# Mixer A's projections by 512 columns, indexer queries for 384 tokens, and the norm's squares shared with GpSimd

## The chip, the cores and the metric

The kernel runs on one core of a Trainium2 chip. What counts is the device time of one execution in microseconds (us). Three runs of the kernel before gave 1569.32, 1564.32 and 1567.81 us; the median is 1567.81 us. The core has five engines, each with its own queue of instructions: PE (TensorE: matmuls, and the transposes that are written as matmuls), DVE (VectorE), ACT (ScalarE), POOL (GpSimd) and SP (SyncE, which issues transfers here). PE's weight loads are shown apart from its matmuls, as PEld.

## The reference

Two layers of a transformer trunk on 512 tokens of width 1024, in fp32. Cut to what the change touches:

```
for l in range(2):
    h = rms_norm(x, norm_mix[l])                       # the "mixing norm"
    z = h @ w_in[l]
    qa, ka, va, qi, ki, wi, cq, ckv, kr, ga, gb = split_cols(z)
    # mixer A: 8 heads of 64; q and k are normed per head
    # indexer: I[t,s] = sum_h w[t,h] * relu(qi[t,h] . ki[s]); the best 128 keys of each query are kept
    y_a = sparse_indexed_attention(rms_norm(qa), rms_norm(ka), va, qi, ki, wi, rel_bias, topk=128)
    y_b = latent_attention(...)                        # mixer B: low-rank q and kv, 8 heads
    x = x + (sigmoid(ga) * (y_a @ w_proj_a) + sigmoid(gb) * (y_b @ w_proj_b)) @ w_out
    h = rms_norm(x, norm_ffn[l])
    x = x + (silu(gate) * val of causal_dwconv(h @ w_up)) @ w_down
```

A query of the first 128 tokens can see at most 128 keys, as many as are kept, so for these tokens the choice of the best keys leaves nothing out.

## The kernel before, in words

Each fp32 product is computed as three matmuls: both operands are split into a rounded high part and a low part (the rest), and the products high by high, low by high and high by low are summed in a PSUM bank. The activations' parts are called `hxh` and `hxl` (L295 on ACT, L296 on DVE).

**Weights** come as tiles of 128 rows and up to 1152 columns, in the order of one long list (`plan`). A tile passes through four steps: a transfer into `wr` (three buffers, issued by SP), the high part `wh` by a copy on ACT (L168), and the low part `wl`, either by a subtraction on DVE (L177) or, for the names in the set `DL`, by a negated copy on ACT (L193) and an accumulating transfer that POOL issues (L194). `wh` and `wl` have four buffers each. `get` hands out a tile's parts; `ahead`, called at the end of each tile's matmuls, starts the next tiles. The tiles `dn` of the down projection go through three more sums on POOL and DVE (L203 to L205), because the down projection is done with seven products of half the size instead of eight.

**A layer** is laid out around attention. The start of a layer is `lat`: the indexer queries in four tiles `qi` of 128 columns (two heads each), the first two of them interleaved by k while the norm's operands still arrive (L316 to L318), the next two through `dense` (L512), then `kiw` (the indexer's keys and head weights), `ckv` and `cq`. The evacuation of a `qi` tile (`stack`) is two copies on ACT (L301, L302) and two subtractions on DVE (L305, L306), and these free the PSUM bank. The mixing norm's sum of squares is made beside that: ACT squares the eight tiles of x (L446), DVE adds the squares up one after the other (L450), and four tiny matmuls on ones (L456) sum over the partitions; DVE's L461 goes on from there.

Then attention runs, first the indexer's scores and the choice of keys together with mixer B, then mixer A. Between its small steps PE gets *filler*: dense projections from a generator (`mix_dense`), handed out a few matmuls at a time at a rate set in the code; `later(n, f)` puts f off by n such steps. The filler's order is the order of the weight list: `gb`, `kv`, `uq`, then mixer A's projections `qa`, `ka`, `va` of heads 0 to 3 (`a0`), some `ga`, the same for heads 4 to 7 (`a1`), then `pb`, more `ga`, `pa`. `rows` computes a projection by token: the activations of 128 tokens are the stationary operand, and 256 columns of weights are streamed (L535). A weight tile holds four k slices of 256 columns; two PSUM banks take two token blocks each. There are 3 names x 2 groups x 96 = 576 such matmuls in a layer.

After mixer A come the output projection, the second norm, and the feed-forward in two halves: `uv` and `ug` (up projection, with the convolution), then `dn`. A group `mp` of down products ends with the residual sums: ACT's L1385, DVE's L1386 to L1392 write x. In layer 0 the next layer's first operands `hxh` wait for the last of them. A scheduler reorders the instructions of each engine from the traced program; the PSUM banks are D (2), L (3), T (2) and Y (1).

Of the kernel before, what the change touches and what calls it, by code (L numbers as in the profile page):

```python
# [10 lines left out]
F32 = mybir.dt.float32  # L11
# [8 lines left out]
D = 1024  # L20
# [8 lines left out]
TOPK = 128  # L29
IDX_SCALE = (8 ** -0.5) * (64 ** -0.5)  # L30
# [68 lines left out]
def dense_plan():  # L99
# [28 lines left out]
class Weights:  # L128


    def __init__(self, nc, wd, pool, slot, later):
# [8 lines left out]
        self.at = 2  # L140
# [13 lines left out]
    def split(self, i, lag=0):  # L154
        if i >= len(self.seq) or i in self.parts:
            return
# [12 lines left out]
        if name in DL:  # L169
            self.low_by_dma(t[:, :n], o[:, :n])  # L170
            return
# [42 lines left out]
    def ahead(self):  # L214

        for j in range(1, WB[1]):
            self.split(self.at + j, 2)
        for j in range(WB[1], WB[1] + WB[0] - 1):
            self.load(self.at + j)
        if PRE and self.at + WB[1] < len(self.seq) and self.seq[self.at + WB[1]][0] == "dn":  # L220
            self.sums(self.at + WB[1], self.raw[self.at + WB[1]])
# [3 lines left out]
def trunk(ctx: ExitStack, tc: tile.TileContext, xT, wd, vecs, rel, rot_n, onehot, outT):  # L225
# [72 lines left out]
    def stack(p, name):  # L298

        e, o = slot(name + "e", F32R), slot(name + "o", F32R)  # L300
        A.copy(e[0:64], p[0:64])  # L301
        A.copy(o[64:128], p[64:128])  # L302

        def low():
            V.tensor_tensor(out=e[64:128], in0=p[0:64], in1=e[0:64].bitcast(F32), op=OP.subtract)  # L305
            V.tensor_tensor(out=o[0:64], in0=p[64:128], in1=o[64:128].bitcast(F32), op=OP.subtract)  # L306
# [13 lines left out]
    def rsqrt(a, shape, quick=False):  # L320

        y, t = small("y", shape), small("t", shape)
# [88 lines left out]
    def late_consts():  # L411
# [7 lines left out]
        for n, w in ((0, 512), (1, 128)):  # L419
# [5 lines left out]
        nc.scalar.dma_start(bass.AP(tensor=dst.tensor, offset=dst.offset, ap=[[5120, 128], [640, 8], [1, 640]]),  # L425
                            bass.AP(tensor=src.tensor, offset=src.offset, ap=[[0, 128], [640, 8], [1, 640]]))
# [7 lines left out]
    class Norm:  # L434
        def __init__(self, gain):
            self.gain = gain
# [64 lines left out]
    def dense(kt, parts, xh, xl, evac, c0=0, last=True, tag="D"):  # L501
# [7 lines left out]
        for n, (w, x) in enumerate(seq):  # L509
            if n and n % 3 == 0:  # L510
                yield
            mm(p, lhsT=w, rhs=x, start=n == 0, stop=n == len(seq) - 1, skip_group_check=True)  # L512
# [5 lines left out]
    def rows(name, grp, nrm, evac):  # L518
# [1007 lines left out]
```

## Time and profile before

| | us |
|---|---|
| median of three runs | 1567.81 (1564.32 to 1569.32) |
| the profiled execution | 1562.11 |
| its span | 1560.4 |
| PE busy | 1542.9 (99%) |
| DVE busy | 1116.3 (72%) |
| ACT busy | 950.4 (61%) |
| POOL busy | 414.5 (27%) |

The profile is of one execution, whose time lies 1.7 us above its span. Busy shares are averages over a program in stages, so a table by stretches of the span says more than the whole. Matmuls overlap in PE's pipeline: the duration of a row is not what it costs. What a row of matmuls costs is the distance from one start to the next, called the cadence below. A note in brackets behind a row says how long the engine stood idle ahead of it and what it had waited for. The granted clock of TensorE is 1.00 in every stretch.

### The profile page before, as it was taken

Reading aid. Unit: us, or ns where it says so; the run is one execution under the profiler, and the core shown is the slowest. Engines: PE = TensorE matmul, PEld = TensorE weight load, DVE = VectorE, ACT = ScalarE, POOL = GpSimd, SP = SyncE. Lnnn points to the kernel's source line nnn. Section 1 sums busy time; section 2 is a strip of 40 time slices with the busy share of each in tenths; the row PEclk is TensorE's granted clock in tenths of the full one; section 3 lists DMA queues with packets and bytes.
Section 4 is the critical chain, followed back from the end, with each engine's and each line's share of the span. In section 5 each row is a group of like instructions: output and inputs, shape, how many; then the busy total and the mean of one; then the engine's idle time right before and its main releaser. Section 6 shows DMA issues by size and latency. Waiting matters only on the chain.

```text
span 1560.4 us, 23953 instructions
## 1 busy us (share of the span) xinstructions
PE 1542.9 (99%) x8662; PEld 1338.8 (86%) x8662; DVE 1116.3 (72%) x2271; ACT 950.4 (61%) x1551; POOL 414.5 (27%) x602
## 2 busy tenths in 40 slices
PE   9999999999999999999999999999999999999998
PEld 6888999888888898889978879998888888988898
DVE  7799988666476682548778999886574757735576
ACT  6757677773577545664457666687635764356642
POOL 1234003300011231217802430124000113412276
PEclk9999999999999999999999999999999999999999
DMA  7573134743578439983444732247435783499833
GB/s 238 150 183 96 55 95 100 184 126 118 128 187 190 109 106 212 215 190 88 142 149 110 171 97 62 84 123 174 145 98 140 185 190 94 114 209 209 198 101 102
DMA packets 72263, 221.11 MB, mean 142 GB/s; under 512 B 8448, under 2 KB 8744, under 8 KB 72016
## 3 DMA queue, kind: packets, MB, share of 16 engines
q1 hardware_dynamic: 53248, 149.41, 30.9%
q0 software_dynamic: 18432, 67.38, 23.3%
q10 hardware_dynamic: 464, 2.79, 0.6%
q8 instruction: 68, 1.11, 0.3%
q14 instruction: 51, 0.42, 0.1%
HBM read 143.77 MB, written 6.84 MB: 97 GB/s over the span
## 4 chain that ended last, share of the span: by engine, by line
PE 69%; DVE 10%; POOL 4%; DMA 4%; ACT 3%; issue 2%; POOLq 0%; DVEq 0%; ACTq 0%; SPq 0%
PE D L512 37%; PE T L512 14%; PE D L535 6%; DMA wr<-in_wd_dram 2%; PE Y L1033 2%; POOL wr L205 2%; PE T L1026 2%; DVE wl L188 2%; DMA wl<-wr 1%; PE L L1373 1%; POOL wr L204 1%; PE L L313 1%; POOL wr L203 1%; PE L L312 1%; ACT wh L183 1%
## 5 line engine op out<-in xcount | busy, mean ns | idle before, releaser
L168 ACT CAST wh<-wr 128x1024 fp32r<-128x1024 f32 x202 | 211.9, 1051 | 177.7 <-PE D L512 67.1
L194 POOL DMA_DIRECT2D wl<-wr x128 | 110.8, 873 | 646.4 <-ACT wl L193 596.3
L512 PE MATMUL D<-hxh,wh 128*128 128x512 f32 x464 | 185.2, 399 | 0.4 <-DVE qio L306 0.4
L512 PE MATMUL D<-hxl,wh 128*128 128x512 f32 x464 | 183.5, 396 | 0.0
L183 ACT CAST wh<-wr 128x896 fp32r<-128x896 f32 x88 | 82.8, 942 | 127.4 <-POOL wr L205 99.5
L193 ACT ACTIVATE wl<-wr 128x1024 fp32r<-128x1024 f32 (+1 forms) x128 | 135.7, 1060 | 26.6 <-PE D L512 19.6
L205 POOL TENSOR_TENSOR wr<-wr 128x256 f32<-128x256 f32 x88 | 108.1, 1228 | 92.1 <-DVE wr L204 76.6
L188 DVE TENSOR_TENSOR wl<-wr,wh 128x896 fp32r<-128x896 f32 x88 | 102.0, 1160 | 40.4 <-ACT wh L183 36.0
L1068 POOL TENSOR_TENSOR P<-M,sel 128x128 f32<-128x128 f32 (+1 forms) x64 | 54.4, 903 | 274.4 <-DMA M<-skewd 229.7
L512 PE MATMUL D<-hxh,wl 128*128 128x512 f32 x464 | 126.1, 397 | 0.0
L535 PE MATMUL D<-wh,hxh 128*128 128x256 f32 x384 | 114.0, 298 | 0.0
L535 PE MATMUL D<-wl,hxh 128*128 128x256 f32 x384 | 108.9, 284 | 0.0
L535 PE MATMUL D<-wh,hxl 128*128 128x256 f32 x384 | 108.4, 283 | 0.0
L512 PEld LDWEIGHTS D<-hxh,wh 128*128 128x128 f32 x464 | 87.5, 189 | 15.7 <-issue 0.8
L177 DVE TENSOR_TENSOR wl<-wr,wh 128x1024 fp32r<-128x1024 f32 x74 | 92.0, 1246 | 11.5 <-ACT wh L168 9.2
L512 PEld LDWEIGHTS D<-hxl,wh 128*128 128x128 f32 x464 | 87.4, 188 | 14.4
L512 PE MATMUL D<-hrl,wh 128*128 128x512 f32 x256 | 99.6, 389 | 0.0
L512 PE MATMUL D<-hrh,wh 128*128 128x512 f32 x256 | 99.6, 389 | 0.0
L512 PE MATMUL T<-hrh,wh 128*128 128x512 f32 x256 | 99.6, 389 | 0.0
L512 PE MATMUL T<-hrl,wh 128*128 128x512 f32 x256 | 99.6, 389 | 0.0
L512 PEld LDWEIGHTS D<-hxh,wl 128*128 128x128 f32 x464 | 84.4, 188 | 15.4 <-issue 0.2
L293 DVE TENSOR_TENSOR ptl<-T,pth 128x512 fp32r<-128x512 f32 (+3 forms) x128 | 60.9, 484 | 21.8 <-ACT pth L292 20.7
(395 smaller groups left out, 4516.5 us busy)
## 6 DMA issues: line engine op xcount, KB each, us to landing
wr<-in_wd_dram SPq DMA_DIRECT2D x198, 512.0 KB, 4.1
wl<-wr POOLq DMA_DIRECT2D x124, 512.0 KB, 5.6
wr<-in_wd_dram SPq DMA_DIRECT2D x88, 256.0 KB, 2.7
x<-in_xT_dram SPq DMA_DIRECT2D x16, 256.0 KB, 4.2
M<-skewd SPq DMA_DIRECT2D x16, 256.0 KB, 4.0
skewd<-biasd ACTq DMA_DIRECT2D x1, 2560.0 KB, 13.6
wr<-in_wd_dram SPq DMA_DIRECT2D x4, 576.0 KB, 3.9
wl<-wr POOLq DMA_DIRECT2D x4, 576.0 KB, 6.1
```

The lines of the kernel that those rows point to most:

```text
L168: self.nc.scalar.copy(h[:, :n], t[:, :n])
L177: eng.tensor_tensor(out=o[:, c], in0=t[:, c], in1=h[:, c].bitcast(F32), op=OP.subtract)
L183: self.nc.scalar.copy(h[:, :896], t[:, 128:1024])
L188: self.later(lag, lambda: self.nc.vector.tensor_tensor(out=o[:, :896], in0=t[:, 128:1024], in1=h[:, :896].bitcast(F32), op=OP.subtract))
L193: self.nc.scalar.activation(o, t, AF.Copy, scale=-1.0)
L194: self.nc.gpsimd.dma_start(o.bitcast(F32), t, accum_op=OP.add)
L205: g(2)(out=b[:, 6:8], in0=b[:, 0:3:2], in1=b[:, 3:6:2], op=OP.add)
L293: later(lag, lambda: V.tensor_tensor(out=o, in0=src, in1=h.bitcast(F32), op=OP.subtract))
L512: mm(p, lhsT=w, rhs=x, start=n == 0, stop=n == len(seq) - 1, skip_group_check=True)
L535: mm(pp[b][:, t, :], lhsT=x, rhs=w, start=n == 0 and half == 0 and t == 0, stop=n == 11 and half == 1, skip_group_check=True)
L1026: nc.tensor.transpose(p[:, (i - j) * 128:(i - j + 1) * 128], P[:, P0[i] + j * 128:P0[i] + (j + 1) * 128], ident)
L1068: G.tensor_tensor(out=P[:, P0[i]:P0[i] + w], in0=M[:, 512 - w:512], in1=sel[:, SEL0[i]:SEL0[i] + w], op=OP.add)
```

## The change

1. `rows` streams 512 columns. The weights are packed anew: `qk` holds q and k of four heads (2 x 256 columns), four tiles of two k slices; `va` holds v of all heads and is made once. All four tiles of a projection are fetched ahead of its first matmul, a PSUM bank takes one token block, and the tiles are given back during the last of the four token blocks. A layer has 3 x 96 = 288 such matmuls. `a0` is now `qk` and `va`, `a1` is `qk` alone.
2. The indexer queries are made for tokens 128 to 511: 384 columns a matmul (192 matmuls over both layers), and `stack` copies 384 columns.
3. The mixing norm's squares 5 to 7 are added to square 4 on POOL, which also adds the two sums; DVE keeps the adds of squares 1 to 3.
4. The transfer of the bias table `skewd` (2560 KB, issued by ACT) is put off by 36 steps.
5. The first two tiles behind a run of `dn` tiles (`uv` and `ug` with index 10, in each layer) get their low part from DVE.
6. `held`: at the last two pairs of tiles of the group mp = 3, in layer 0, the next tiles' work is written behind the residual sums instead of ahead of them.
7. The per-head norm of mixer A's q and k is one chain of [128, 4, 8] per group of heads instead of two of [128, 16] (q, k).

```diff
-    for g in range(2):
-        p += [(n, 2 * g + half, 1024) for n in ("qa", "ka", "va") for half in range(2)]
-        if g == 0:
-            p += [("ga", m, 1024) for m in range(GA_0)]
+    p += [("qk", i, 1024) for i in range(4)] + [("va", i, 1024) for i in range(4)]
+    p += [("ga", m, 1024) for m in range(GA_0)]
+    p += [("qk", 4 + i, 1024) for i in range(4)]
...
-        if name in DL:
+        if name in DL and not any(self.seq[j][0] == "dn" for j in (i - 1, i - 2)):
...
-    def rows(name, grp, nrm, evac):
-        pp = [bank("D").rearrange("p (t c) -> p t c", t=2) for _ in range(2)]
-        for half in range(2):
-            h, o = W.get(name, 2 * grp + half)
-            for b in range(2):
-                for t in range(2):
...
+    def rows(name, i0, nrm, evac):
+        parts = [W.get(name, i0 + i) for i in range(4)]
+        for t in range(4):
+            p = bank("D")
+            ts = slice(t * 128, (t + 1) * 128)
+            for i, (h, o) in enumerate(parts):
+                c = lambda k: slice(k * 512, (k + 1) * 512)
+                xs = [(nrm.h[2 * i + k][:, ts], nrm.o[2 * i + k][:, ts]) for k in range(2)]
+                seq = [(x, h[:, c(k)]) for k in range(2) for x in xs[k]] + [(xs[k][0], o[:, c(k)]) for k in range(2)]
+                for n, (x, w) in enumerate(seq):
+                    if n == 3:
+                        yield
+                    mm(p, lhsT=x, rhs=w, start=i == 0 and n == 0, stop=i == 3 and n == 5, skip_group_check=True)
+                if t == 3:
                     W.ahead()
...
-                mm3(p, h, o, nrm.h[k], nrm.o[k], k == 0, k == KD - 1)
+                mm3(p[:, T_IDX:], h, o, nrm.h[k][:, T_IDX:], nrm.o[k][:, T_IDX:], k == 0, k == KD - 1)
...
-                later(lag, lambda: V.tensor_tensor(out=self.acc, in0=self.acc, in1=q, op=OP.add))
+                def add():
+                    if k < 4 or not self.two:
+                        V.tensor_tensor(out=self.acc, in0=self.acc, in1=q, op=OP.add)
+                    else:
+                        G.tensor_tensor(out=self.acc2, in0=self.acc2, in1=q, op=OP.add)
+                    if k == KD - 1 and self.two:
+                        G.tensor_tensor(out=self.acc, in0=self.acc, in1=self.acc2, op=OP.add)
+                later(lag, add)
...
-                W.ahead()
+                held = last and mp == 3 and l < DEPTH - 1 and kp in pairs[-2:]
+                if held:
+                    W.split(W.at + 1, 2)
+                else:
+                    W.ahead()
...
+            if held:
+                W.ahead(2)
```

What the scheduler makes of it, at three places. The first is PE's queue at the norm's sum in layer 0, first before, then after. `D_402` (after: `D_401`) is the bank of `kiw`, `D_334` that of the fourth `qi` tile, `relb` is the operand of the bias table, and the matmuls on `ones` are the norm's sum.

```order
L512 MATMUL D_334<-hxh_175,wl_198 128x512
L421 MATMUL T_362<-oh_356,relb 8x512
L421 MATMUL T_366<-oh_357,relb 8x128
L512 MATMUL D_334<-hxh_179,wl_198 128x512
...
L512 MATMUL D_402<-hxh_143,wh_308 128x512
...
L512 MATMUL D_402<-hxl_160,wh_308 128x512
L456 MATMUL T_410<-ones,sq_228 128x1 x4
```

```order
L528 MATMUL D_333<-hxh_187,wl_198 128x384
L528 MATMUL D_401<-hxh_143,wh_307 128x512
...
L528 MATMUL D_401<-hxh_171,wh_307 128x512
L427 MATMUL T_362<-oh_356,relb 8x512
L427 MATMUL T_366<-oh_357,relb 8x128
L528 MATMUL D_401<-hxl_172,wh_307 128x512
L528 MATMUL D_401<-hxh_175,wh_307 128x512
L528 MATMUL D_401<-hxl_176,wh_307 128x512
L472 MATMUL T_409<-ones,sq_228 128x1 x4
```

The bias table's matmuls moved from the tail of the last `qi` tile into `kiw`, and the norm's sum comes after ten matmuls of `kiw` instead of six. It now waits for POOL, whose queue after the change has these rows at that place (`sq_228` is the sum, `sq_290` the second sum).

```order
L463 TENSOR_TENSOR sq_290<-sq_290,sq_298 128x512
L463 TENSOR_TENSOR sq_290<-sq_290,sq_328 128x512
L463 TENSOR_TENSOR sq_290<-sq_290,sq_343 128x512
L465 TENSOR_TENSOR sq_228<-sq_228,sq_290 128x512
L597 TENSOR_TENSOR w_81_502<-wn_500,r_82_503 128x32
```

On DVE's queue in layer 0 four of the seven adds are gone, and the low part of a third weight tile now stands ahead of the subtractions that free the second-last `qi` bank, where before it stood behind them.

The second place is ACT's queue at the boundary from layer 0 to layer 1, first before, then after. `t_8294` (after: `t_7963`) is the first of the last residual sums, `hxh` are the next layer's operands; the numbers of the names grow in the order in which the code asks for buffers.

```order
L168 CAST wh_8196<-wr_8138 128x1024
L168 CAST wh_8224<-wr_8170 128x1024
L168 CAST wh_8262<-wr_8199 128x1024
L168 CAST wh_8289<-wr_8227 128x1024
L1385 COPY t_8294<-D_8108 128x256
L295 ACTIVATE hxh_8304<-x_4394,vec 128x512
```

```order
L168 CAST wh_7876<-wr_7818 128x1024
L168 CAST wh_7904<-wr_7850 128x1024
L168 CAST wh_7981<-wr_7879 128x1024
L168 CAST wh_7984<-wr_7907 128x1024
L1394 COPY t_7963<-D_7788 128x256
L297 ACTIVATE hxh_7973<-x_4076,vec 128x512
```

The names show that the two last casts are now asked for behind the residual sum (7981 and 7984 against 7963), but they stand where they stood. The same holds on DVE for their low parts, and on SP for the transfers. The transfer of the bias table has moved by one row of ACT's queue: it stood one row ahead of a weight cast and now stands one row behind it.

The third place is ACT's queue behind the first half's `dn` tiles in layer 0, first before, then after. `wr_6332` and `wr_6376` (after: `wr_6023`, `wr_6058`) are the `uv` and `ug` tiles with index 10.

```order
L183 CAST wh_6373<-wr_6301 128x896
L168 CAST wh_6400<-wr_6332 128x1024
L193 ACTIVATE wl_6401<-wr_6332 128x1024
L168 CAST wh_6428<-wr_6376 128x1024
L193 ACTIVATE wl_6429<-wr_6376 128x1024
L168 CAST wh_6456<-wr_6405 128x1024
L193 ACTIVATE wl_6457<-wr_6405 128x1024
```

```order
L184 CAST wh_6055<-wr_6021 128x896
L168 CAST wh_6082<-wr_6023 128x1024
L168 CAST wh_6109<-wr_6058 128x1024
L168 CAST wh_6136<-wr_6085 128x1024
L194 ACTIVATE wl_6137<-wr_6085 128x1024
```

Two negated copies are gone from ACT, and with them two accumulating transfers from POOL's queue; DVE has two subtractions more there.

Elsewhere on PE the filler moves with the shorter projections: in layer 0 mixer B's last scores end at row 991 of PE's queue instead of 1119, mixer A's first scores begin at row 1062 instead of 1166, and the eight score matmuls of mixer A's last head, which had filler between them, stand together at rows 1530 to 1537, with `pb` behind them.

## Rows read from the trace of the kernel before

**Rows 1.** The page's part 1: busy time, share of the span, instructions.

```profile
PE 1542.9 (99%) x8662; PEld 1338.8 (86%) x8662; DVE 1116.3 (72%) x2271; ACT 950.4 (61%) x1551; POOL 414.5 (27%) x602
```

**Rows 2.** Busy time by stretches of the span; last clock, DMA share, GB/s.

```profile
core 0: us, PE busy (x) PEld busy (x) DVE busy (x) ACT busy (x) POOL busy (x), PEclk, DMA share, GB/s
61.00:184.00 123.00, 121.76 (x674) 103.96 (x672) 120.69 (x350) 81.30 (x166) 34.70 (x85) 1.00 0.47 118
184.00:274.00 90.00, 89.21 (x705) 86.15 (x705) 75.80 (x187) 66.95 (x143) 17.20 (x19) 1.00 0.35 94
760.00:794.00 34.00, 30.24 (x196) 26.17 (x195) 25.89 (x33) 15.49 (x21) 15.29 (x17) 1.00 0.57 186
```

**Rows 3.** Two stretches, of line L535 (the projections by token) alone.

```profile
184.00:274.00 90.00, 68.94 (x480) 61.72 (x480) 1.00 0.35 94
960.00:1049.00 89.00, 68.96 (x480) 61.82 (x480) 1.00 0.34 91
```

**Rows 4.** Timeline of PE: start, duration; matmuls of 256, 512 and 384 columns.

```profile
232.08 0.28 PE L535 MATMUL D<-wh,hxl 128*128 128x256 f32 x1
...
233.04 0.28 PE L535 MATMUL D<-wh,hxh 128*128 128x256 f32 x1
...
335.20 0.39 PE L512 MATMUL D<-ybl,wh 128*128 128x512 f32 x1
...
336.11 0.39 PE L512 MATMUL D<-ybl,wh 128*128 128x512 f32 x1
...
107.73 0.33 PE L844 MATMUL L<-wl,cqh 128*128 128x384 f32 x1
...
108.59 0.33 PE L844 MATMUL L<-wh,cql 128*128 128x384 f32 x1
```

**Rows 5.** Timeline of PE at the start of layer 0.

```profile
11.61 0.50 PE L317 MATMUL L<-hxl,wh 128*128 128x512 f32 x1 [0.28 <-DVE hxl L296]
...
18.36 0.39 PE L512 MATMUL D<-hxh,wh 128*128 128x512 f32 x1
...
28.65 1.24 PE L421 MATMUL T<-oh,relb 32*8 32x512 f32 x4
...
30.62 0.39 PE L512 MATMUL D<-hxh,wh 128*128 128x512 f32 x1
...
31.99 0.95 PE L456 MATMUL T<-ones,sq 128*128 128x1 f32 x8
32.80 0.49 PE L512 MATMUL D<-hxh,wh 128*128 128x512 f32 x1
```

**Rows 6.** Timeline of DVE at the start of layer 0.

```profile
28.55 0.69 DVE L306 TENSOR_TENSOR qio<-D,qio 64x512 fp32r<-64x512 f32 x1
...
30.42 0.68 DVE L450 TENSOR_TENSOR sq<-sq,sq 128x512 f32<-128x512 f32 x1
```

**Rows 7.** Timeline of PE at the boundary of the layers.

```profile
791.81 0.50 PE L316 MATMUL L<-hxh,wh 128*128 128x512 f32 x1 [1.70 <-ACT hxh L295]
...
806.71 0.47 PE L512 MATMUL D<-hxh,wh 128*128 128x512 f32 x1 [0.40 <-DVE qio L306]
```

**Rows 8.** Timeline of ACT at the boundary of the layers.

```profile
791.03 1.33 ACT L295 ACTIVATE hxh<-x,vec 128x512 fp32r<-128x512 f32 x2 [4.54 <-DVE x L1389]
...
803.51 0.63 ACT L446 ACTIVATE sq<-x 128x512 f32<-128x512 f32 x1
```

**Rows 9.** Timeline of PE behind the `dn` tiles of both layers.

```profile
590.52 1.65 PE L512 MATMUL D<-hrh,wl 128*128 128x512 f32 x6 [0.80 <-DMA wl<-wr]
...
1366.46 1.88 PE L512 MATMUL D<-hrh,wl 128*128 128x512 f32 x7 [0.59 <-DMA wl<-wr]
```

**Rows 10.** Groups of instructions by line and shape: busy, mean ns, idle before.

```profile
L631 POOL TENSOR_TENSOR sqc<-sqc,sqc 128x512 f32<-128x512 f32 x2 | 3.0, 1476 | 0.0
...
L450 DVE TENSOR_TENSOR sq<-sq,sq 128x512 f32<-128x512 f32 x28 | 19.3, 688 | 0.7 <-ACT sq L446 0.2
```

**Rows 11.** The page's part 5, columns as in rows 10: a weight tile's two splits.

```profile
L168 ACT CAST wh<-wr 128x1024 fp32r<-128x1024 f32 x202 | 211.9, 1051 | 177.7 <-PE D L512 67.1
...
L177 DVE TENSOR_TENSOR wl<-wr,wh 128x1024 fp32r<-128x1024 f32 x74 | 92.0, 1246 | 11.5 <-ACT wh L168 9.2
```

**Rows 12.** The page's part 6, DMA issues: KB each, median us to landing.

```profile
wr<-in_wd_dram SPq DMA_DIRECT2D x198, 512.0 KB, 4.1
wl<-wr POOLq DMA_DIRECT2D x124, 512.0 KB, 5.6
```

More of the change, by code (lines that the diff above doesn't have):

```diff
@@ L212, in get, with ahead @@
         return self.parts.pop(i)
-    def ahead(self):
+    def ahead(self, n=1):
+        self.used += n
         for j in range(1, WB[1]):
-            self.split(self.at + j, 2)
+            self.split(self.used + j, 2)
         for j in range(WB[1], WB[1] + WB[0] - 1):
-            self.load(self.at + j)
-        if PRE and self.at + WB[1] < len(self.seq) and self.seq[self.at + WB[1]][0] == "dn":
-            self.sums(self.at + WB[1], self.raw[self.at + WB[1]])
+            self.load(self.used + j)
+        if PRE and self.used + WB[1] < len(self.seq) and self.seq[self.used + WB[1]][0] == "dn":
+            self.sums(self.used + WB[1], self.raw[self.used + WB[1]])
 @with_exitstack
@@ L320, in rsqrt @@
     def rsqrt(a, shape, quick=False):
-        y, t = small("y", shape), small("t", shape)
+        if int(np.prod(shape)) > 16:
+            y, t = (sb.tile([128] + shape, F32, name=nm("y"), tag="heads", bufs=4) for _ in range(2))
+        else:
+            y, t = small("y", shape), small("t", shape)
         V.tensor_scalar(y.bitcast(I32), a.bitcast(I32), -0.5, float(0x5F3759DF), op0=OP.mult, op1=OP.add)
@@ L434, in trunk, with __init__ @@
     class Norm:
-        def __init__(self, gain):
-            self.gain = gain
+        def __init__(self, gain, two=False):
+            self.gain, self.two = gain, two
             self.h, self.o = [None] * KD, [None] * KD
@@ L498, in spread, with dense @@
             A.copy(row, p)
-    def dense(kt, parts, xh, xl, evac, c0=0, last=True, tag="D"):
+    def dense(kt, parts, xh, xl, evac, c0=0, last=True, tag="D", t0=0):
         h, o = parts
@@ L706, in mix_dense, with heads, evac @@
         done.add("latent")
-        def heads(name, grp, gain):
-            ss = small("ss", [16])
+        def heads(grp, gain):
+            ss = sb.tile([128, 4, 8], F32, name=nm("ss"), tag="heads", bufs=4)
             nat = []
-            def evac(b, p):
-                p = p.rearrange("p t c -> p (t c)")
+            def evac(t, p):
                 r, q = slot("raw"), slot("sqa")
@@ L745, in turn @@
                 hd = 4 * grp + 2 * pr
-                if gain is None:
-                    st["qa"][hd:hd + 2] = stack(p, name)
+                if not keys:
+                    st["qa"][hd:hd + 2] = stack(p, "qa")
                     return
@@ L1375, in down @@
                         tick()
-                W.ahead()
+                held = last and mp == 3 and l < DEPTH - 1 and kp in pairs[-2:]
+                if held:
+                    W.split(W.at + 1, 2)
+                else:
+                    W.ahead()
                 tick()
```

109 lines of the change are left out of this document (50 added, 59 removed).

## The prediction

> **What bounds the kernel.** I read the page's part 1 first: PE is busy for 1542.9 us of the span [rows 1], so time can only come from three places: matmuls that cost less, the few stalls between them, or stretches in which PE only fills the time of another engine. Then the table by stretches tells these apart [rows 2]. In 184 to 274 us PE is busy for 89.21 of 90 us and DVE for 75.80: PE is the limit. In 61 to 184 us (choice of keys, mixer B) DVE is busy for 120.69 of 123 us: PE's filler is free cover there, and a matmul less saves nothing by itself. In 760 to 794 us (boundary of the layers) PE has 30.24 of 34 us; a chain of waits decides. Last came the timeline, for the distance between starts of matmuls [rows 4]: 256 columns 0.120 us ((233.04 - 232.08) / 8), 384 columns 0.172 us (0.86 / 5), 512 columns 0.2275 us (0.91 / 4). The cost per column falls only a little with more columns.
>
> **The projections by token.** They stream the same columns in half as many matmuls. Two of 256 cost 0.240 us, one of 512 costs 0.2275 us: 12.5 ns for each pair. The change counts where PE is the limit. The two such stretches hold 480 of a layer's 576 instructions each [rows 3]; the other 96 lie where DVE is the limit and give nothing. So 2 x 240 x 12.5 ns = 6.0 us is saved. If the 96 count too it is 7.2 us.
>
> A rule bears on this and would make the term smaller. The rows show 12.5 ns a pair [rows 4]. The Trainium skill (TensorE: Matmul & The Clock Gate, Back-to-back issue gap) puts the isolated distance of warm matmuls at columns / 2.4 plus 2.5 ns, by which 256 and 512 columns take 109.2 and 215.8 ns, and a pair saves 2.5 ns: an estimate by that page is 1.2 us instead of 6.0. The trace's distances lie above both figures, and the smaller form lies further above; I keep the rows.
>
> The new form asks for four tiles at once. Each tile takes ACT 1.05 us and DVE 1.25 us [rows 11]. The tiles are given back one by one in the last token block, 6 x 0.2275 = 1.4 us apart, so the splits of the next four can follow at that pace, and the first has 18 x 0.2275 = 4.1 us from its release to its use, against 2.3 us for the two splits. I cost this at nothing; the cover is the raw tile already landed, and what it costs without that is a rival below.
>
> The shorter filler shifts all that follows, as the order shows: mixer A's last head has no filler between its eight scores. PE would then wait for a bank to be freed now and then. The nearest row is a wait of 0.40 us for DVE to free a bank [rows 7]; two in a layer are 0.8 us. From 0 to 1.5 us a layer is possible; I add 1.5 us for both.
>
> **The indexer queries.** 96 matmuls a layer go from 512 to 384 columns, 55 ns each: 5.3 us a layer at most. At the start of layer 0 not all of it is worth something. PE waits for the operands' low parts until 11.61 us [rows 5]; of the first 48 matmuls some 28 stand behind that wait, and with the 48 of the next two tiles 76 x 55 ns = 4.2 us are saved by the time `kiw` begins. It would then begin at 30.62 - 4.2 = 26.4 us [rows 5], and 1.2 us earlier still since the bias table's matmuls (1.17 us) have moved into it. But it needs the bank that DVE's subtraction frees at 28.55 + 0.69 = 29.24 us [rows 6]. There DVE has three adds of 0.69 us less ahead and one split of 1.25 us more [rows 10, 11]: 28.4 us. From 28.4 us `kiw` takes 24 x 0.2275 = 5.5 us, the norm's sum 0.8 us and the bias table 1.2 us: it ends at 35.9 us. Before, it ended at 30.62 + 5.5 + 0.8 = 36.9 us. So layer 0 saves **1.0 us**; bounds are 0 and 4.2.
>
> At layer 1 the operands of the last two k slices come late: PE waits 1.70 us for `hxh` at 791.81 us [rows 7], and this operand ends a chain through ACT and DVE in which ACT idles 4.54 us for the last residual sum [rows 8]. All that PE saves ahead of it is waited away. Behind it stand 12 of the first 48 matmuls (0.7 us). Then `kiw` begins at 806.71 us, after a wait for DVE [rows 7], in whose queue three adds ahead go away: 2.1 us earlier. Together 2.7 us, less half of a possible wait of 0.8 us for the norm's sum (next paragraph): **2.3 us**, bounds 0.7 and 5.3.
>
> **The squares.** Eight of DVE's adds (0.69 us each) become eight of POOL's, for which 1.48 us is the nearest row [rows 10]. DVE's gain is in the bank's release above. The chain's end moves: after the last square, POOL needs up to two adds, 3.0 us. In layer 1 the last square ends at 803.51 + 0.63 = 804.1 us [rows 8], perhaps 0.9 us earlier now, so the sum is ready near 806.2 to 807.1 us, and the norm's sum, ten matmuls into `kiw`, comes at 804.4 + 2.3 = 806.7 us. In layer 0 it comes at 28.4 + 2.3 + 1.2 = 31.9 us; DVE's last add began at 30.42 us [rows 6], and POOL's ends near 31.4. Behind it on PE stands the rest of `kiw`. Hence the 0.4 us charged in layer 1. If POOL's adds take longer, PE waits by as much.
>
> On the chip's side: the Trainium skill (GPSIMD Engine Reference, Key points) says that GpSimd shares its interfaces to SBUF with VectorE and that instructions with two SBUF inputs contend; the adds have two each. No row here shows such an add beside DVE's splits, so that is left to a rival.
>
> **The tiles after `dn`.** PE waits for the accumulating transfer at 590.52 us (0.80 us) and at 1366.46 us (0.59 us) [rows 9]. The chain is ACT's copies and a transfer of 5.6 us [rows 12]; DVE's subtraction takes 1.25 us [rows 11]. I count the whole **1.4 us**; DVE's queue behind the residual sums could keep half.
>
> **The rest at nothing.** `held` changes no row of ACT's, DVE's or SP's order at the boundary, so the late operand there stays late. The bias table's transfer moves one row. The shorter norm per head saves DVE some short instructions where PE is the limit.
>
> **The sum.** -6.0 - 1.0 - 2.3 - 1.4 + 1.5 = -9.2 us. The profiled execution took 1562.1 us, 5.7 us under the median 1567.8 us of the runs shown. It becomes 1552.9 us; put against the median, **1558.6 us**.
>
> **The rivals.**
> - *Every matmul counts.* The filler in the stretches of DVE and the queries at both starts all shorten the way: 7.2 + 10.6 + 1.4 = 19.2 us, 1548.6 us. For it: PE is busy for 99%. Against it: three waits by name in rows 5 and 7.
> - *The starts take all of the queries' gain.* POOL's adds run 1 us longer each, as the norm's sum then waits, or the bank is freed no earlier: -6.0 - 1.4 + 1.5 = -5.9 us, 1561.9 us.
> - *Wider matmuls give nothing much.* The distance between starts would be set by columns alone, so that two of 256 cost nearly one of 512: PE's rows of 256 columns would shrink to their share whatever their number. The rows at 232 us speak against it, though they stand in a mixed stretch. With 1.2 us for the projections in place of 6.0 the sum is -4.4 us: 1563.4 us. This is the skill's rule above (TensorE: Matmul & The Clock Gate), as a mechanism.
> - *The moved work acts as written.* If the two casts did run behind the residual sums, PE's 1.70 us wait and the other stalls of a stretch with 30.24 of 34 us busy shrink [rows 2], by up to 4 us: 1555 us. The order speaks against it.
> - *Slower: four tiles at once starve PE.* Where a tile has not landed when its block begins, transfer (4.1 us [rows 12]) and splits (1.05 + 1.25 us) lie bare, 6.4 us. There are three blocks a layer, and the tiles behind them. To undo the sum and reach slower, six starts would have to lose (9.2 + 4.7) / 6 = 2.3 us each. At half of 6.4 us each the loss is 19.2 us: 1567.8 - 9.2 + 19.2 = 1577.8 us. For it: DVE is busy for 84% of that stretch (75.80 of 90, [rows 2]), so that its splits queue. Against it: the releases above, and transfers at a share of 0.35.
>
> **Chances and range.** A measurement tells about 0.3%, 4.7 us, from no change: 1563.1 to 1572.5 us. The forecast 0.52 (its own range 1554 to 1562), every matmul 0.10, moved work 0.05, the starts take all 0.15 (a fifth of it within 0.3%), wider matmuls little 0.08 (on the bound; within), starved PE 0.10 (0.03 within, 0.07 slower). Faster: 0.52 + 0.10 + 0.05 + 0.12 - 0.03 for the scatter of runs = 0.76; within 0.17; slower 0.07. The range leaves out most of the starved case and little else: 1548 to 1566 us.
>
> **What would show it.** The projections' starts 0.2275 us apart in a stretch shorter by 3 us a layer; `kiw` beginning near 28.4 us and 2 us earlier behind the boundary; no wait for `wl` behind the `dn` tiles; the wait for `hxh` at the boundary still there, and longer. The prediction is wrong if rows of `wh` or `wl` from ACT and DVE appear as PE's waits at the first matmul of a projection, if the norm's sum waits for POOL by over 2 us, or if the stretch of mixer A does not shorten though its matmuls do.

## The result and the profile after

Nine runs of the changed kernel had a median of 1577.11 us (1571.41 to 1581.13), nine of the kernel before 1567.81 us (1562.73 to 1571.94). The ratio is 1.0068, with a 95% interval of 1.0055 to 1.0081: 9.3 us slower by the medians, where 9.2 us faster was forecast. The profiled execution took 1575.77 us with a span of 1572.9 us, 12.5 us more than before. The two profiles are not alike in their luck: that of before (1562.11 us, its mean granted clock 1.000) is faster than each of the nine runs, that of after lies near the median. So the table below shows where time is lost, and overstates by some 3 us how much.

The page's part 1 after the change [rows 1]:

```profile
PE 1540.0 (98%) x8086; PEld 1310.1 (83%) x8086; DVE 1105.4 (70%) x2223; ACT 945.8 (60%) x1547; POOL 425.6 (27%) x606
```

PE has 576 instructions less and hardly less busy time. Part of its busy time ran at half the clock, and the rest of the loss is idle time. To find the places I took the same landmarks in both timelines: the first index score, the first projection of mixer A's output (the `ya` matmuls), the start of layer 1, and the same in layer 1.

| from, to | before, us | after, us | difference |
|---|---|---|---|
| 0, first index score | 45.56 | 49.57 | +4.0 |
| first index score, first `ya` (attention) | 313.86 | 319.72 | +5.9 |
| first `ya`, layer 1 (output, feed-forward) | 421.17 | 418.42 | -2.8 |
| layer 1, first index score | 39.79 | 38.97 | -0.8 |
| first index score, first `ya` | 314.80 | 321.72 | +6.9 |
| first `ya`, last matmul | 419.33 | 418.65 | -0.7 |

**The start of layer 0.** PE's timeline after the change (start, duration, in brackets the idle ahead) answers to [rows 5]:

```profile
28.42 0.47 PE L528 MATMUL D<-hxh,wh 128*128 128x512 f32 x1 [2.40 <-DVE qio L309]
...
29.20 0.39 PE L528 MATMUL D<-hxl,wh 128*128 128x512 f32 x1
29.42 0.58 PE L528 MATMUL D<-hxh,wh 128*128 128x512 f32 x1
29.80 0.63 PE L528 MATMUL D<-hxl,wh 128*128 128x512 f32 x1
...
30.79 2.30 PE L427 MATMUL T<-oh,relb 32*8 32x512 f32 x4
...
34.46 1.70 PE L472 MATMUL T<-ones,sq 128*128 128x1 f32 x8
...
37.02 0.63 PE L528 MATMUL D<-hxh,wh 128*128 128x512 f32 x1
37.45 0.63 PE L528 MATMUL D<-hxl,wh 128*128 128x512 f32 x1
...
41.03 0.39 PE L528 MATMUL D<-hxh,wh 128*128 128x512 f32 x1
```

`kiw` begins at 28.42 us, and waits 2.40 us for the bank, as worked out (28.4 us). But behind 29.8 us the starts of such matmuls lie 0.43 us apart (37.02 and 37.45 us) instead of 0.23. The table by stretches (PE, PEld, DVE, ACT and POOL busy, then granted clock, DMA share, GB/s) shows why:

```profile
15.00:25.00 10.00, 10.00 (x60) 10.00 (x59) 8.64 (x11) 9.13 (x16) 4.67 (x7) 1.00 0.51 163
25.00:29.00 4.00, 1.60 (x9) 1.22 (x9) 3.23 (x4) 2.74 (x5) 2.25 (x2) 1.00 0.74 217
29.00:31.00 2.00, 2.00 (x7) 1.05 (x6) 1.35 (x1) 0.32 (x1) 1.92 (x2) 0.62 0.86 330
31.00:39.00 8.00, 8.00 (x22) 5.39 (x21) 2.45 (x14) 1.71 (x5) 0.82 (x1) 0.50 0.24 75
39.00:41.00 2.00, 2.00 (x8) 1.58 (x8) 0.83 (x3) 1.01 (x1) 0.00 (x0) 0.82 0.60 164
41.00:46.00 5.00, 5.00 (x25) 4.14 (x24) 1.62 (x2) 1.57 (x3) 0.00 (x0) 1.00 1.03 283
```

Behind the idle the granted clock is 0.50, the lower of TensorE's two levels, for about ten us. In that stretch a busy share of 100% hides the loss: what a matmul costs is read from the starts and the clock.

**Attention.** PE has two waits of over 1 us in each layer here. The first is where the last projection `qk` begins, shown on DVE and then on PE:

```profile
237.50 1.23 DVE L178 TENSOR_TENSOR wl<-wr,wh 128x1024 fp32r<-128x1024 f32 x1 [0.76 <-ACT wh L168]
...
239.47 1.23 DVE L178 TENSOR_TENSOR wl<-wr,wh 128x1024 fp32r<-128x1024 f32 x1
...
241.21 1.22 DVE L178 TENSOR_TENSOR wl<-wr,wh 128x1024 fp32r<-128x1024 f32 x1
242.35 1.65 DVE L298 SCALAR_TENSOR_TENSOR va<-D,rstd,va 128x256 fp32r<-128x256 f32 x4
```

```profile
243.36 0.47 PE L547 MATMUL D<-wh,hxh 128*128 128x512 f32 x1 [1.27 <-DVE va L298]
```

DVE is given the low parts of the next four tiles in a burst, and three of them stand ahead of the subtractions that empty the two banks of `va`. The second wait is behind that projection, when the first `ga` tiles are wanted (in both kernels all of `ga` follows the last projection, and `pb` follows `ga`). First come POOL's accumulating transfer for the first `ga` tile with its time to landing and SP's next two issues, then ACT's queue, then PE's:

```profile
266.94 0.86 POOL L195 DMA_DIRECT2D wl<-wr  x1 [9.93 <-ACT pth L294]
```

```profile
wl<-wr POOLq DMA_DIRECT2D x1, 512.0 KB, 4.6
```

```profile
271.56 0.33 SPq L151 DMA_DIRECT2D wr<-in_wd_dram  x1
...
274.73 0.33 SPq L151 DMA_DIRECT2D wr<-in_wd_dram  x1
```

```profile
270.17 1.06 ACT L194 ACTIVATE wl<-wr 128x1024 fp32r<-128x1024 f32 x1
...
277.54 1.04 ACT L168 CAST wh<-wr 128x1024 fp32r<-128x1024 f32 x1 [4.35 <-DMA wr<-in_wd_dram]
278.49 1.05 ACT L194 ACTIVATE wl<-wr 128x1024 fp32r<-128x1024 f32 x1
279.45 0.60 ACT L352 ACTIVATE P<-P,mx 128x384 f32<-128x384 f32 x1
279.96 0.19 ACT L352 ACTIVATION_READ_ACCUMULATOR P<-P,mx 128x1 f32 x1
280.05 0.56 ACT L294 CAST pth<-T 128x512 fp32r<-128x512 f32 x1
```

```profile
280.66 0.50 PE L1038 MATMUL Y<-pth,va 128*128 128x512 f32 x1 [3.48 <-ACT pth L294]
...
282.29 0.63 PE L528 MATMUL D<-hxl,wh 128*128 128x512 f32 x1
```

ACT's cast of the fourth `ga` tile waits 4.35 us for its transfer, issued only at 271.56 us, when the accumulating transfer that read the first tile's raw buffer had landed (266.94 us and 4.6 us). Behind that cast in ACT's queue stand the negated copy of the same tile, an exponent of the softmax and the cast `pth` that PE needs. The list of waits names `pth`; the cause stands four rows higher. PE idles for 3.48 us, and from 281.9 to 285.1 us its starts too lie 0.43 us apart.

**The boundary** answers to [rows 7]:

```profile
799.23 0.62 PE L319 MATMUL L<-hxh,wh 128*128 128x384 f32 x2 [3.67 <-ACT hxh L297]
...
812.06 0.47 PE L528 MATMUL D<-hxh,wh 128*128 128x512 f32 x1 [2.06 <-ACT qio L305]
...
814.36 1.05 PE L472 MATMUL T<-ones,sq 128*128 128x1 f32 x8 [0.68 <-POOL sq L465]
```

The wait for `hxh` is 3.67 us instead of 1.70, and `kiw` waits for its bank here too. The clock stays at 1.00 behind both in this execution. That is the exception: in the profiles of e1 to e4, e6 to e9 and e11 below, PE waits 2.85 to 4.46 us here and the clock falls during or behind each of these waits. So it is in e1 (the row of the wait, and 798 to 802 us at 0.50):

```profile
796.79 0.69 PE L319 MATMUL L<-hxh,wh 128*128 128x384 f32 x1 [3.44 <-ACT hxh L297]
```

```profile
798.00:802.00 4.00, 4.00 (x14) 4.00 (x13) 2.05 (x4) 2.47 (x4) 0.00 (x0) 0.50 0.00 0
```

### The profile page after: what moved, and what is told of

Its sections match the earlier page's. It is cut to its first block, busy times and chain, and to the rows that moved or that the text cites. A ratio compares the mean times of both kernels' runs of the same rounds, so it can differ in the third digit from the quotient of the medians.

```text
span 1572.9 us, 22741 instructions
## 1 busy us (share of the span) xinstructions
PE 1540.0 (98%) x8086; PEld 1310.1 (83%) x8086; DVE 1105.4 (70%) x2223; ACT 945.8 (60%) x1547; POOL 425.6 (27%) x606
## 4 chain that ended last, share of the span: by engine, by line
PE 72%; DVE 7%; POOL 5%; issue 4%; DMA 3%; ACT 2%; SPq 0%; POOLq 0%; DVEq 0%; ACTq 0%
PE D L528 36%; PE T L528 15%; PE D L547 4%; PE L L1378 3%; PE Y L1038 2%; PE T L1378 2%; PE T L1031 2%; POOL wr L206 2%; DMA wr<-in_wd_dram 2%; PE D L1378 1%; PE L L528 1%; PE Y L1378 1%; POOL wr L205 1%; POOL wr L204 1%; DVE wl L178 1%
## 5 line engine op out<-in xcount | busy, mean ns | idle before, releaser
L195 POOL DMA_DIRECT2D wl<-wr x124 | 107.4, 866 | 691.9 <-ACT wl L194 608.4
L528 PE MATMUL D<-hxh,wh 128*128 128x512 f32 (+1 forms) x464 | 186.7, 402 | 4.5 <-DVE qio L309 2.4
L528 PE MATMUL D<-hxl,wh 128*128 128x512 f32 (+1 forms) x464 | 185.1, 399 | 0.0
L194 ACT ACTIVATE wl<-wr 128x1024 fp32r<-128x1024 f32 x124 | 131.7, 1062 | 34.2 <-PE D L528 20.1
L206 POOL TENSOR_TENSOR wr<-wr 128x256 f32<-128x256 f32 x88 | 114.5, 1302 | 90.5 <-DVE wr L205 83.0
L528 PE MATMUL D<-hxh,wl 128*128 128x512 f32 (+1 forms) x464 | 125.5, 395 | 0.0
L178 DVE TENSOR_TENSOR wl<-wr,wh 128x1024 fp32r<-128x1024 f32 x78 | 97.6, 1258 | 13.2 <-ACT wh L168 8.7
L547 PE MATMUL D<-wh,hxh 128*128 128x512 f32 x192 | 78.7, 410 | 2.5 <-DVE va L298 2.5
L1324 DVE SCALAR_TENSOR_TENSOR c<-T,vec,c 128x511 f32<-128x511 f32 x32 | 23.9, 748 | 80.2 <-ACT c L1321 80.2
L547 PE MATMUL D<-wh,hxl 128*128 128x512 f32 x192 | 77.9, 406 | 0.0
```

Source lines behind the costliest of these rows:

```text
L178: eng.tensor_tensor(out=o[:, c], in0=t[:, c], in1=h[:, c].bitcast(F32), op=OP.subtract)
L194: self.nc.scalar.activation(o, t, AF.Copy, scale=-1.0)
L195: self.nc.gpsimd.dma_start(o.bitcast(F32), t, accum_op=OP.add)
L206: g(2)(out=b[:, 6:8], in0=b[:, 0:3:2], in1=b[:, 3:6:2], op=OP.add)
L528: mm(p[:, t0:], lhsT=w, rhs=x[:, t0:], start=n == 0, stop=n == len(seq) - 1, skip_group_check=True)
L547: mm(p, lhsT=x, rhs=w, start=i == 0 and n == 0, stop=i == 3 and n == 5, skip_group_check=True)
```

## The experiments

Two causes are to be told apart from others: at the start, an idle that the shorter queries open, and a clock that falls behind it; in attention, the burst of weight tiles. Each experiment was timed in five rounds against the kernel before, whose own median was 1565.59 us beside e1 to e4, 1566.20 us beside e5 to e8 and 1567.04 us beside e9 to e12; so ratios are compared, not medians. The intervals of e1, e2, e5, e6, e8 and e11 overlap that of the changed kernel: what these show, they show by the waits, the landmarks and the clock of one profile each. In the table "score" is the time of layer 0's first index score in the profile (45.56 us before the change, 49.57 after), and "clock" that of the stretch from 31 to 39 us.

| run | median, us | ratio to before, 95% interval | score | clock |
|---|---|---|---|---|
| changed kernel | 1577.11 | 1.0068 (1.0055 to 1.0081) | 49.57 | 0.50 |
| e1 cover | 1574.30 | 1.0052 (1.0039 to 1.0066) | 45.46 | 1.00 |
| e2 `kiw` in bank Y | 1580.46 | 1.0090 (1.0074 to 1.0105) | 51.29 | 0.63 |
| e3 `ga` by DVE | 1568.06 | 1.0012 (0.9999 to 1.0026) | 49.67 | 0.50 |
| e4 old projections | 1563.05 | 0.9980 (0.9967 to 0.9993) | 45.42 | 1.00 |
| e5 queries of 512 | 1575.10 | 1.0054 (1.0036 to 1.0072) | 45.70 | 1.00 |
| e6 sum on PE | 1573.65 | 1.0043 (1.0026 to 1.0060) | 49.37 | 0.57 |
| e7 e4 and e6 | 1564.49 | 0.9989 (0.9975 to 1.0003) | 47.38 | 0.79 |
| e8 `uv` as before | 1576.62 | 1.0062 (1.0040 to 1.0085) | 50.50 | 0.50 |
| e9 e3 and e5 | 1565.33 | 0.9993 (0.9982 to 1.0004) | 46.10 | 1.00 |
| e10 e4 and e5 | 1560.61 | 0.9967 (0.9953 to 0.9980) | 45.65 | 1.00 |
| e11 squares on DVE | 1577.65 | 1.0068 (1.0053 to 1.0084) | 49.64 | 0.50 |
| e12 `uv` alone | 1562.26 | 0.9971 (0.9959 to 0.9983) | 46.26 | 1.00 |

**e1, cover.** Matmuls without use fill the idle ahead of `kiw`.

```diff
+        if l == 0:
+            pw = bank("Y")
+            for k in range(10):
+                mm(pw, lhsT=wi[1][:, k % 8 * 128:k % 8 * 128 + 128], rhs=nrm.h[k % 8], start=True, stop=True)
         yield from dense(KD, W.get("kiw", 0), nrm.h, nrm.o, lambda p: nrm.after(lambda: evac_kiw(p)))
```

> Ten more matmuls of 512 columns into an unused bank stand ahead of kiw in layer 0; their results are not used. They fill the 2.40 us in which PE waited for kiw's bank at 26.0 us; kiw can begin no earlier than before. Theory (the idle lowered the granted clock): the clock stays at full speed behind 28.4 us, the first index score comes near 45.5 us instead of 49.57 us, and the time falls by about 4 us against the changed kernel, to about 1573 us (ratio to the kernel before near 1.004). Rival (the clock fell for another reason, such as the transfers or the small bias-table matmuls): the first index score stays near 49.5 us and the time near 1577 us. Neither expects anything of mixer A.

PE's timeline in e1, and the stretch that was at 0.50:

```profile
25.01 2.47 PE L714 MATMUL Y<-hxh,wl 128*128 128x512 f32 x10
27.41 1.24 PE L427 MATMUL T<-oh,relb 32*8 32x512 f32 x4
28.58 0.50 PE L528 MATMUL D<-hxh,wh 128*128 128x512 f32 x1
```

```profile
31.00:39.00 8.00, 7.18 (x36) 6.11 (x37) 4.50 (x17) 1.82 (x3) 0.76 (x1) 1.00 0.88 281
```

`kiw` begins no earlier (28.58 us), the clock stays at 1.00, and the score comes 4.1 us earlier although more work was added. The ratio falls by 0.0016, or 2.5 us, which is not clear of the noise; the span of the profile is only 0.9 us shorter, since the clock falls at the boundary here (above). The bias table's matmuls also stand ahead of `kiw` here, which the edit did not aim at.

**e2, `kiw` in bank Y**, so that no wait for DVE is left.

```diff
-        yield from dense(KD, W.get("kiw", 0), nrm.h, nrm.o, lambda p: nrm.after(lambda: evac_kiw(p)))
+        yield from dense(KD, W.get("kiw", 0), nrm.h, nrm.o, lambda p: nrm.after(lambda: evac_kiw(p)), tag="Y")
```

> The changed kernel with kiw's sum in the bank tagged Y instead of D, in both layers, so that kiw needs no bank freed by DVE. Theory (the bank's release is what PE waits for, and the clock falls behind that idle): kiw begins at 26.1 us instead of 28.4 us, the clock stays at full speed, the first index score comes near 42.5 us instead of 49.57 us; at layer 1 the 2.06 us wait at 812.06 us is gone. Together 8 to 9 us less: about 1568.5 us, ratio to the kernel before 1.000 to 1.002. Rival (the norm's sum on POOL is the true end): kiw begins earlier but PE waits for POOL's add, and only 2 to 3 us are gained.

The rival was nearer, and even it hoped for too much:

```profile
32.60 1.46 PE L472 MATMUL T<-ones,sq 128*128 128x1 f32 x8 [1.55 <-POOL sq L465]
...
34.50 0.63 PE L528 MATMUL Y<-hxh,wh 128*128 128x512 f32 x1
```

The idle moves to the norm's sum, and the clock falls there. POOL's last add ends at 32.5 us (30.42 us and 2.12 us); no earlier start of `kiw` changes that.

**e3, the first `ga` tiles by DVE.**

```diff
-        if name in DL and not any(self.seq[j][0] == "dn" for j in (i - 1, i - 2)):
+        if name in DL and not any(self.seq[j][0] in ("dn", "qk", "va") for j in (i - 1, i - 2)):
```

> The changed kernel with the low parts of the first two ga tiles behind mixer A's last projection made by DVE instead of by ACT and an accumulating transfer, in both layers. Theory (the raw buffers are held by the accumulating transfers, the fourth ga tile lands late, and ACT's cast that waits 4.35 us for it holds up the exponent and the copies behind it in ACT's queue): the wait of 3.48 us at 280.66 us is gone, the clock does not fall there, and each layer gains 4 to 5.5 us: about 1567 us, ratio near 1.000. Rival (mixer A is longer because its own chain has less filler beside it): the wait moves to another place of mixer A, the stage from the last projection to the first ya projection keeps within 2 us of its 99.8 us, and the time is over 1574 us.

```profile
277.75 0.39 PE L1038 MATMUL Y<-pth,va 128*128 128x512 f32 x1
278.29 0.50 PE L1038 MATMUL Y<-ptl,va 128*128 128x512 f32 x1 [0.15 <-DVE ptl L295]
```

```profile
274.00:280.00 6.00, 5.85 (x28) 4.48 (x27) 5.53 (x17) 4.66 (x11) 3.86 (x5) 1.00 0.59 148
280.00:286.00 6.00, 6.00 (x35) 5.13 (x34) 5.43 (x15) 4.04 (x9) 0.86 (x1) 1.00 0.97 180
```

The wait of 3.48 us is gone in both layers, the clock holds (0.72 in 280 to 286 us after the change), and the time falls by 9 us. DVE's subtraction for the first `ga` tile and SP's next issue are these:

```profile
266.40 1.23 DVE L178 TENSOR_TENSOR wl<-wr,wh 128x1024 fp32r<-128x1024 f32 x1 [0.19 <-ACT wh L168]
```

```profile
267.66 0.33 SPq L151 DMA_DIRECT2D wr<-in_wd_dram  x1
```

The raw buffer that DVE has read (266.40 us and 1.23 us) is given to the next transfer 0.03 us later; the one that the accumulating transfer still read in the changed kernel was given on at 271.56 us.

**e4, mixer A's projections as before**, all else changed.

```diff
-    p += [("qk", i, 1024) for i in range(4)] + [("va", i, 1024) for i in range(4)]
+    for g in range(2):
+        p += [(n, 2 * g + half, 1024) for n in ("qa", "ka", "va") for half in range(2)]
...
-    def rows(name, i0, nrm, evac):
+    def rows(name, grp, nrm, evac):
```

> The changed kernel with mixer A's projections as before (256 columns, three names, two halves, the weights packed as before, the per-head norm as before); all else changed. Theory (of the 9.3 us lost, 12.8 us are lost in mixer A of the two layers): mixer A's stages take as long as before the change, and the time is 12 to 13 us under the changed kernel, 1564 to 1565 us, ratio 0.997 to 0.999. Rival (the projections by 512 columns are a gain by themselves and mixer A is late because the layer starts late): the time stays near 1577 us or rises.

As the theory says, 14 us less. The two attention stages take 313.57 and 315.06 us, as before the change. The start holds a surprise:

```profile
28.61 0.47 PE L529 MATMUL D<-hxh,wh 128*128 128x512 f32 x1 [3.20 <-DVE qio L310]
```

```profile
31.00:39.00 8.00, 7.81 (x38) 5.97 (x37) 4.44 (x17) 2.74 (x5) 1.01 (x1) 1.00 0.62 203
```

The idle is there, longer than in the changed kernel, and the clock did not fall behind it in this execution. So a fall behind such an idle is likely, not certain: of the profiles here with over 2 us of idle ahead of `kiw`, four show it (the changed kernel, e3, e8, e11) and one does not; of those with at most 1.6 us of idle up to the norm's sum and only its eight rows there (before, e1, e5, e9, e10, e12) none does, but e2 with 1.55 us does.

**e5, queries for all tokens.**

```diff
-T_IDX = TOPK
+T_IDX = 0
```

> The changed kernel with the indexer queries made for all 512 tokens again (512 columns, full stacks). Theory (the shorter queries leave PE with nothing to do between 26.0 and 28.4 us, and the clock falls behind that): PE is busy until kiw's bank is free, the wait ahead of kiw is under 0.6 us, the clock stays at full speed to 46 us, the first index score comes at 45 to 46.5 us instead of 49.57 us. Layer 1's start is as long as before the change. In all 2 to 4 us under the changed kernel, 1573 to 1575 us, although PE has 192 longer matmuls (10.6 us more of matmul time). Rival (matmul time counts): 5 to 10 us over the changed kernel, 1582 to 1587 us.

PE has no wait between 24 and 33 us, the clock holds, the score comes at 45.70 us: the theory's signs. In time it is 0.0014 of the ratio, 2 us, at the lower end of the forecast and within the noise. In these profiles the shorter matmuls made the start longer. At layer 1 the start takes 39.13 us, as good as the changed kernel's 38.97: the shorter queries saved next to nothing there.

**e6, the sum of squares on PE**, with e2's edit; **e7**, both with e4's.

```diff
-                    if k == KD - 1 and self.two:
-                        G.tensor_tensor(out=self.acc, in0=self.acc, in1=self.acc2, op=OP.add)
...
+                if self.two:
+                    mm(p[:, i:i + 1], lhsT=self.acc2[:, i * 128:(i + 1) * 128], rhs=ones[:, 0:1], start=False,
+                       stop=True)
```

> As e2 (kiw's sum in bank Y), and POOL's last add of the two sums of squares is left out: PE sums both with eight small matmuls on ones instead of four. Theory (at the start PE waits first for kiw's bank, and with that gone for POOL's last add of 2.12 us; behind either idle the clock falls): no wait above 0.5 us between 26 and 36 us, clock at full speed, first index score at 42.5 to 44 us instead of 49.57 (51.29 in e2); 2 to 3 us at layer 1. Mixer A's loss stays. About 1568 us, ratio 1.000 to 1.003. Rival (the start of a layer is as long as the chain of weights, squares and the norm on the other engines allows): the first index score does not come before 45 us, the time is over 1571 us.

> e4 (mixer A's projections as before) with e6's two edits at the norm. Theory: mixer A as before the change, and a start shorter than before by 2 to 3 us in each layer, the stalls behind dn gone: 1557 to 1560 us, ratio 0.993 to 0.996, faster than both kernels. Rival (as e6's): no better than e4, 1563 us.

My theory failed here. No wait over 0.5 us is left, and the clock falls all the same:

```profile
30.07 0.35 PE L470 MATMUL T<-ones,sq 128*128 128x1 f32 x2 [0.43 <-POOL sq L463]
...
31.98 0.56 PE L473 MATMUL T<-ones,sq 128*128 128x1 f32 x2
32.41 0.77 PE L529 MATMUL Y<-hxl,wh 128*128 128x512 f32 x1
32.98 0.63 PE L529 MATMUL Y<-hxh,wh 128*128 128x512 f32 x1
```

The sixteen rows with a single column take 2.3 us behind a wait of 0.43 us, and PE counts as busy in them. By the distance of the rows' starts (0.22 us, then 0.43 us) the fall comes 1.2 us into them, near 31.3 us; in e7 it comes behind all sixteen and three wide matmuls more, near 32.2 us. What made it fall is not shown, and whether a later place for the sum would have kept the clock was not tried. The start was not made shorter than before in this way; e7 is no better than e4.

**e8, `uv` and `ug` as before; e12, that part alone on the kernel before.**

```diff
-        if name in DL and not any(self.seq[j][0] == "dn" for j in (i - 1, i - 2)):
+        if name in DL:
```

> The changed kernel with the uv and ug tiles behind dn split as before (negated copy on ACT, accumulating transfer). Prediction's term: the two waits for the low part, 0.80 and 0.59 us before the change, come back; 1 to 2 us more than the changed kernel. Rival (the residual sums on DVE hold the new splits, so nothing was gained): no wait for a transfer there and the same time within 0.5 us, or a wait for DVE's low part in the changed kernel.

> The kernel before with one part of the change: the first two tiles behind dn have their low part from DVE. Prediction's term: both waits for the accumulating transfer (0.80 and 0.59 us) gone, 1 to 2 us under the kernel before, 1564 to 1565 us at a median before of 1566, ratio 0.9985 to 0.9995. If the stretch behind is also less disturbed, up to 3 us. Rival: nothing, the wait is put off to the next tile.

In e8 PE waits for the accumulating transfer again, three times and 1.3 us in all; in the changed kernel and in e12 it does so nowhere. e8's time cannot be told from the changed kernel's. e12 is faster than the kernel before by 0.3% (4.8 us between the medians of one session), while its profile is 1.8 us shorter in span than that of before and its fastest run 1.4 us under the fastest of before (1560.30 and 1561.67 us). The term is at least as large as forecast; why the median gains more stays open. The profiles understate it: e12's has a fall of the clock behind its wait of 1.77 us at the boundary, that of before has none behind 1.70 us.

**e9, e3 and e5 together; e10, e4 and e5.**

> The changed kernel with e3's and e5's edits together (first two ga tiles split by DVE, indexer queries for all tokens). If the two causes are the whole of the loss and independent, the gains add: 9 us of e3 and 2 us of e5 (4 where the clock would have fallen by its full length) under the changed kernel: 1564 to 1567 us, ratio 0.998 to 1.001; first index score at 45.7 us, mixer A's stage from the first mixer B transposed tile to the first ya projection at 232 to 233 us in place of 237.5 us (231.3 before the change). Rival (a third cause): over 1569 us.

> e4 with the indexer queries for all tokens: of the change only the split behind dn, the squares on POOL, the later bias table and held are left. Theory: start of layer 0 as before (45.6 us) without the fall of the clock that e4 has in some executions, mixer A as before, the stretch from the first down projection to layer 1 some 2.5 us shorter, layer 1's start 0.5 to 1 us shorter: 1561 to 1563 us, ratio 0.996 to 0.998. Rival (the shorter queries do help where the clock holds, as in e4's profile): not under e4's 1563 us.

e9 takes away both causes by their own remedies and keeps the projections by 512 columns: the loss is gone, the ratio 0.9993. Its attention stages take 314.75 and 317.59 us, 0.9 and 2.8 us over those of before; the 1.27 us waits for `va` are still in them. By the profiles it is still 3.2 us longer than before (1563.6 and 1560.4 us), which again sets a fast execution of before against it. In three pairs (e5 against the changed kernel, e9 against e3, e10 against e4) the ratio is 0.0013 to 0.0019 lower with the queries for all tokens, each within the noise by itself. e10 is the fastest, beats both kernels and lies beside e12, so the squares on POOL and the rest add little.

**e11, the squares all on DVE.**

```diff
-    nrm = Norm(gain0, True)
+    nrm = Norm(gain0)
```

> The changed kernel with the mixing norm's squares all added by DVE again. Theory (the squares on POOL are not what loses the time): the wait ahead of kiw in layer 0 is 1.5 to 3.5 us still and the clock falls behind it, the wait of 0.68 us for POOL's sum at layer 1 is gone; mixer A's stall stays; within 2 us of the changed kernel, 1575 to 1578 us. Rival (POOL's adds lengthen DVE's instructions, or the sum on POOL is what delays the layer): 4 us or more under the changed kernel.

As the theory says: 1577.65 us, a wait of 3.31 us ahead of `kiw`, the clock at 0.50 behind it. The squares on POOL are not the cause of the loss.

## Why the prediction was wrong, by its own steps

- **"I cost this at nothing; the cover is the raw tile already landed"** (four tiles at once) is the step that failed most. The raw tile had not landed: the accumulating transfers of the `ga` tiles held the three buffers (4.6 to 8.8 us each), and ACT's cast waited with the softmax behind it (3.48 us of PE, and the clock). And I looked at when the splits are needed, not at what they delay: three of them in a burst kept DVE from emptying `va`'s banks (1.27 us). The rival "four tiles at once starve PE" had the direction and the place; its price was off: two waits a layer, and neither is for the parts themselves, so that its 1577.8 us lies beside the measured 1577.11 us by luck. Of the signs of being wrong the third came: mixer A's stretch did not shorten though its matmuls did. e4 takes the whole loss away, e3 the larger half.
- **The projections' term, -6.0 us.** The distance of the new matmuls is as forecast: three starts at 229.76, 229.99 and 230.21 us. Summed from start to start over the timelines, without idles, the projections take 72.5 us in layer 0 and 72.6 us in layer 1 before, and 69.8 and 69.9 us in e9: 5.4 us saved, near the 6.0 of the rows. By the formula of the Trainium skill (TensorE: Matmul & The Clock Gate, Back-to-back issue gap) a pair would save 2.5 ns, an estimate of 1.2 us in all, and the trace does not agree. The saving is real, and the waits alone did not eat it: in e9 PE's other matmuls of attention, the same in number, lie further apart by 2.1 and 2.2 us in all, and PE idles 1.5 and 3.3 us more, so that attention is 0.9 and 2.8 us longer than before. Why the others lie further apart stays open.
- **The queries at layer 0, -1.0 us.** The step "from 28.4 us `kiw` takes 24 x 0.2275 us" failed. The start was right to 0.02 us, with some luck: six shorter subtractions on DVE (0.56 instead of 0.69 us each), a wait of DVE for ACT (0.40 us at 23.02 us) and a split that took 1.83 us were left out and nearly cancel. But the idle ahead of it was priced as if it cost only its own length, and at half the clock `kiw` ended at 41.0 us instead of 35.9. Measured: 4.0 us longer.
- **The queries and squares at layer 1, -2.3 us:** -0.8 us. The wait for `hxh` grew as said, 1.70 to 3.67 us. `kiw` waited 2.06 us for its bank and began 24.35 us into the layer instead of 26.12: 1.8 us earlier where 2.7 were added up. The last releases of banks by ACT and DVE lie 0.05 us apart there (811.97 and 811.92 us), and ahead of DVE's stands a split of 2.32 us instead of the usual 1.22 (next point). The norm's sum then waited 0.68 us (0.4 was charged). With queries for all tokens this start is as short (39.13 us in e5, 38.95 in e10, 38.97 here): what was gained is not the queries'.
- **The squares' price.** POOL's adds took 1.29 to 1.69 us, median 1.43, near the 1.48 us taken [rows 10]; the last took 2.12 and 2.35 us. That they would contend with DVE was left to a rival, and it shows. Of DVE's splits, five run beside these adds and take 1.21, 1.23, 1.35, 1.83 and 2.32 us; the 67 with no arithmetic on POOL beside them take 1.19 to 1.23 us. The average over all splits (1258 ns against 1246) hides it. In layer 1, on DVE and then on POOL:

```profile
808.44 2.32 DVE L178 TENSOR_TENSOR wl<-wr,wh 128x1024 fp32r<-128x1024 f32 x1 [0.54 <-ACT wh L168]
...
811.95 1.23 DVE L178 TENSOR_TENSOR wl<-wr,wh 128x1024 fp32r<-128x1024 f32 x1
```

```profile
807.01 2.66 POOL L463 TENSOR_TENSOR sq<-sq,sq 128x512 f32<-128x512 f32 x2 [22.96 <-ACT sq L453]
...
811.96 2.35 POOL L465 TENSOR_TENSOR sq<-sq,sq 128x512 f32<-128x512 f32 x1
```

In these rows either the split is long or the add is. The Trainium skill (GPSIMD Engine Reference, Key points) has it that GpSimd shares its interfaces to SBUF with VectorE and contends with DVE instructions that have two SBUF inputs; the splits have two, and the trace agrees. It did not decide the time: e11 loses as much without such adds.

- **The tiles after `dn`, -1.4 us:** right in place and sign (e8, e12), and the feed-forward stages are the ones that got shorter.
- **`held`, at nothing:** argued from the order alone; no run leaves it out by itself. **The tail, +1.5 us,** was not measured by itself.

## What to carry to other kernels

Where PE waits for another engine's chain, a shorter matmul makes a longer idle, and the granted clock may make the idle dearer than its length: the starts, not the busy share, tell what the stretch behind it costs. Work that fetches several tiles at once delays what stands behind the splits in the in-order queues of ACT and DVE; price what the burst pushes back, and what still holds the buffers that it needs. Take a rival's mechanism through every queue that it enters before giving it a chance of one in ten.

## What the runs showed of the hardware

Behind an idle of 2.40 us ahead of `kiw` TensorE's granted clock went to its lower level for ten us. Ten us at half the clock are five us lost, an estimate from the table by stretches: twice the idle. Behind 3.20 us at the same place it held in another execution (e4), and behind 3.67 us at the layer boundary too (changed kernel). Counted over the timelines of all fourteen profiles from 14 to 1550 us, PE has 29 idles of 2.4 to 4.5 us, and the clock fell during or within 2.1 us behind 26 of them; of the 37 idles of 1.0 to 2.4 us it did so at two (1.55 us in e2, 1.77 us in e12). It also fell 1.2 us into a run of single-column matmuls (e6), with no idle above 0.43 us ahead of it.

A buffer that an accumulating transfer reads was given on when that transfer had landed, 4.6 us behind its issue, and one that DVE's subtraction reads 0.03 us behind the subtraction's end (e3). Beside POOL's sums a split on DVE took up to 2.32 us instead of 1.22, and beside DVE's splits a sum on POOL up to 2.35 us, where others took 1.29 to 1.69.
